# Four pairs of k tiles by seven products in the down groups too, with the buffers that this needs

## The chip, the cores and the metric

The kernel runs on one core of a Trainium2 chip. The metric is the device time of one execution in microseconds (us), the median of several runs. A core has TensorE (PE, with its weight load PEld), VectorE (DVE), ScalarE (ACT), GpSimd (POOL) and SyncE (SP), each with an instruction queue of its own, and 16 DMA engines that they share. SP issues the plain loads here, POOL the transfers that add to what lies in SBUF.

## What is computed

A decoder trunk of two layers over 256 tokens of 2048 features in float32: layer A with native sparse attention, layer B with dilated attention over one shared K/V, both with attention to 256 memory tokens, and each ended by a SwiGLU feed-forward network (FFN) with 5632 hidden features:

```python
def swiglu(h, w_gate, w_up, w_down):
    return (jax.nn.silu(h @ w_gate) * (h @ w_up)) @ w_down

def layer_b(h, ...):          # layer_a alike, with other attention
    ...
    h = h + o                 # o: attention, projected by w_out
    return h + swiglu(rms_norm(h, norm_ffn), w_gate, w_up, w_down)
```

## The kernel before

**Arithmetic.** Each float32 operand is split into a rounded part and a rest (`split`, lines 78 to 85: ScalarE copies to the `hi` tile, VectorE subtracts to the `lo` tile), and a product of two is three matmuls of 128 x 128 by 128 x 512 (`mm3`, lines 87 to 91: hi x hi, hi x lo, lo x hi).

**Groups of the FFN.** The FFN goes through groups that each fill four PSUM banks: two token tiles by two blocks of 512 columns. A gate/up group gives 512 hidden features from 16 k tiles. The eleven of them come in portions of 4, 4 and 3 (`PORTIONS`), and after each portion two down groups take its hidden features (16, 16 or 12 k tiles) to the 2048 outputs and add them to `h`. In layer B the last portion's down part is done without groups. Per layer the order is: b0, b1, b2, b3, two down groups, b4 to b7, two down groups, b8, b9, b10, and the last down part.

**Seven products for eight.** In a group a pair of k tiles is a 2 x 2 product of blocks (token tile x k tile by k tile x column block), which needs eight block products. For the first pairs of a group (`NPX` = 4 in gate/up groups, `NPH` = 3 in the down groups of the first two portions, 2 in those of the last) the kernel takes seven products of sums and differences instead. On the weights' side VectorE and accumulating POOL transfers build the sums from four quarters (`q`, 512 columns for each pair, so 1536 or 2048 columns); on the activations' side `Paired.finish` (lines 281 to 291) builds them once. The other k tiles are plain chunks: one k tile, 12 matmuls, one 512 KB load each (`raw`, four buffers; `whi`, `wlo`, three).

**The interleaving.** `run_groups` runs the plain chunks of one group and, between them, the seven product steps s0 to s6 of the next (`Group.steps`, line 896 on). `spacing(n)` says how many plain chunks stand ahead of each step, by the number n of plain chunks: 16 in b0, which has no pairs, 10 in a down group with three pairs, 8 in a gate/up group. With 8 it is 1, 2, 2, 2, 0, 1, 0. Each step splits its weights to `qhi` and `qlo` (two buffers each) ahead of its matmuls. The quarters lie in three buffers `qa`, `qb`, `qc`; the next group's first quarter goes to `qa`, which is free after the split of s5. `keep` copies a partial sum from PSUM to one of two buffers, and `rest` holds a difference that starts bank 3 in the next group or is added to `h`.

**Turned activations.** `Paired.heads` (lines 309 to 329) transposes the gated product of a gate/up group on TensorE, six ticks into the next group, and puts it into the hidden tile `hThi`/`hTlo`, through a tile `xf` for the pairs (two pairs at once for the first gate/up group of a portion, one for the second, none later). At the entry to an FFN `Paired.turn` (lines 293 to 306) does the same for `h`, one pair at a time, through one buffer `xf`; `residual_block` queues it after a block of the output projection.

**What sets the order.** TensorE's instructions stand in the order written. The other engines' are ordered by the planner from priorities and a cost model; steps wrapped in `urgent` or `high_priority` go ahead. SP's loads go in order, each held until its buffer is free.

Of the kernel before, what the change touches and what calls it, by code (L numbers as in the profile page):

```python
# [8 lines left out]
F32 = mybir.dt.float32  # L9
F32R = mybir.dt.float32r  # L10
BF16 = mybir.dt.bfloat16
AF = mybir.ActivationFunctionType
# [4 lines left out]
P = 128  # L17
T = 256
# [6 lines left out]
NFB = DFF // 512  # L25
PORTIONS = ((0, 4), (4, 8), (8, 11))
NPX = 4
NPH = 3
NSL = 8
XW = NPX * NSL * P + (KT - 2 * NPX) * T  # L30
HW = NPH * NSL * P + (KT - 2 * NPH) * T
# [13 lines left out]
def decoder_trunk(ctx: ExitStack, tc: tile.TileContext, a: dict, out: bass.AP):  # L45
    nc = tc.nc
# [6 lines left out]
    small.tile([P, PADW], F32, name="padw", bufs=1)  # L53
    phase = ctx.enter_context(ExitStack())
    aux_stack = ExitStack()
    fh = fq = fpool = mm_ps = aux_ps = mm_tags = None

    def open_phase(name, mms, auxs):
# [164 lines left out]
        return r  # L223

    def square_sum(ssq, src):
        junk = work.tile([P, 512], F32, tag="rope2", name="junk") if work is not fq else work.tile([P, 512], F32, tag="hb", name="junk", bufs=2)
        nc.scalar.activation(junk, src, AF.Square, accum_out=ssq)

    def new_ssq():
# [29 lines left out]
    class Paired:  # L259
# [33 lines left out]
        def turn(self, nb, k2, spare):  # L293
            k = nb * 4 + k2 * 2
            if k >= 2 * self.npr:
                to_xT(nb, k2, None, self.gain, tuple(v[:, k - 2 * self.npr:k - 2 * self.npr + 2, :].rearrange("p c t -> p (c t)")
                                                     for v in self.R), spare)
                return
            ps = aux_tile(spare)
            for i, (c, tt) in enumerate(((k, 1), (k, 0), (k + 1, 0), (k + 1, 1))):  # L300
                nc.tensor.transpose(ps[:, i * P:(i + 1) * P], h[:, tt, c * P:(c + 1) * P], ident)
            f = fpool.tile([P, 1, 4, P], F32, tag="xf", name="xf")
            for i in range(2):
                nc.scalar.activation(f[:, 0, i * 2:i * 2 + 2, :], ps[:, i * T:(i + 1) * T].rearrange("p (s t) -> p s t", t=P),  # L304
                                     AF.Copy, scale=self.gain(k + i))
            self.finish(k // 2, 1, f)

        def heads(self, j, tok):

            n = min(max(self.npr - 2 * j, 0), 2)  # L310
            fs = []

            def step(tt):
                ps = aux_tile(tt == 1)
                for i in range(4):
                    nc.tensor.transpose(ps[:, i * P:(i + 1) * P], tok[tt][:, i * P:(i + 1) * P], ident)  # L316
                if n > 0:
                    if tt == 0:
                        fs.append(fpool.tile([P, 2, 4, P], F32, tag="xf", name="xf")[:, :n])
                    f = fs[0]  # L320
                    nc.scalar.activation(f[:, :, 1:3, :] if tt == 0 else f[:, :, 0:4:3, :],
                                         ps[:, :n * T].rearrange("p (q c t) -> p q c t", q=n, t=P), AF.Copy)
                    if tt == 1:
                        self.finish(2 * j, n, f)
                if n < 2:
                    r0 = 4 * j + 2 * n - 2 * self.npr
                    d = tuple(v[:, r0:r0 + 4 - 2 * n, tt * P:(tt + 1) * P] for v in self.R)
                    split(d[0], d[1], ps[:, n * T:].rearrange("p (c t) -> p c t", t=P))

            return [urgent(lambda tt=tt: step(tt)) for tt in range(2)]  # L330
# [514 lines left out]
        return op, finish_rstd(ssq, 4)  # L845

    fpool = p2
    fx, f_r = project_out("a_w_out", KT, 6, 2)
    sub.close()
    stack.close()  # L850
# [2 lines left out]
    class Group:  # L853
# [33 lines left out]
        def fetch(self):  # L887
            self.qa = self.load(0)

        def keep(self, b):  # L890
            t = fq.tile([P, 512], F32, tag="keep", name="keep", bufs=2)
            with tc.high_priority(offset=URGENT):
                nc.scalar.activation(t, self.bank[b], AF.Copy)
            return t

        def steps(self, side):
            def s0():
                if self.qa is None:
                    self.fetch()
                self.new(1)  # L900
                self.product(1, 1, self.qa, side, True)
                with tc.high_priority(offset=URGENT):
                    nc.scalar.activation(self.new(0), self.bank[1], AF.Copy)

            def s1():
                self.qb = self.load(1)
                nc.vector.tensor_add(self.qa, self.qa, self.qb)
                self.new(2)
                self.product(2, 7, self.qa, side, True)
                nc.gpsimd.dma_start(self.qb, self.q[2], accum_op=ALU.add)  # L910
                self.p5 = self.keep(2)

            def s2():
                self.qc = self.load(2)
                nc.vector.tensor_add(self.qa, self.qa, self.qc)
                self.product(1, 5, self.qa, side)
                nc.gpsimd.dma_start(self.qa, self.q[3], accum_op=ALU.add)
                u2 = self.keep(1)
                with tc.high_priority(offset=URGENT):
                    nc.vector.tensor_sub(self.bank[2], self.bank[2], u2)  # L920

            def s3():
                self.product(1, 4, self.qb, side)
                self.r = fq.tile([P, 512], F32, tag="rest", name="rest")
                with tc.high_priority(offset=URGENT):
                    nc.vector.tensor_sub(self.r, self.p5, self.bank[1])
                if self.rest_done is not None:
                    self.rest_done(self)

            def s4():  # L930
                self.product(2, 6, self.qc, side)

            def s5():
                self.qb = self.load(3)
                self.product(1, 3, self.qa, side)

            def s6():
                self.product(0, 2, self.qb, side)

            return [s0, s1, s2, s3, s4, s5, s6]  # L940
# [19 lines left out]
    def spacing(n):  # L960


        return {16: (4, 3, 3, 3, 1, 2, 0), 10: (2, 2, 2, 2, 1, 1, 0), 8: (1, 2, 2, 2, 0, 1, 0)}[n]

    def run_groups(groups):
        for i, g in enumerate(groups):
# [23 lines left out]
    def ffn(pre, op, f_r, last):  # L990
        gq, gs = a[pre + "_gu_q"], a[pre + "_gu_s"]
        groups = []
        for pi, (b0, b1) in enumerate(PORTIONS):
            final = pi == len(PORTIONS) - 1
            nk = 4 * (b1 - b0)
            hp = {}

            def hop(pi=pi, nk=nk, final=final, hp=hp):
                if "op" not in hp:
                    x = pair(lambda i: fh.tile([P, HW], F32R, tag=("hThi", "hTlo")[i], name=("hThi", "hTlo")[i]))  # L1000
                    hp["op"] = Paired(x, NPH - final, nk, sums=not (final and pre == "b"))
                return hp["op"]

            def gate_up(g, j, hop=hop):
                hb = []
                for tt in range(2):
                    t = work.tile([P, 512], F32, tag="hb", name="hb", bufs=2)
                    nc.scalar.activation(t, g.bank[tt], AF.Silu, scale=f_r[:, tt:tt + 1])
                    nc.vector.scalar_tensor_tensor(t, g.bank[2 + tt], f_r[:, tt:tt + 1], t, op0=ALU.mult, op1=ALU.mult)
                    hb.append(t)  # L1010
                deferred.extend(at(hop().heads(j, hb), 6, 6))
# [7 lines left out]
            if final and pre == "b":  # L1019
                run_groups(groups)  # L1020
                last([[a["b_w_down_last"][nb, c] for c in range(nk // CK)] for nb in range(4)], hop().xs, nk)
                return
            npr = NPH - final
            dq, ds = a[f"{pre}_dn_q{pi}"], a[f"{pre}_dn_s{pi}"]
            for n2 in range(2):
                def rest_done(g, n2=n2):
# [137 lines left out]
    for j in range(4):  # L1164
# [8 lines left out]
        deferred.extend(at(heads_T(tok, qT), 4, 7))  # L1173
        deferred.extend(at(dil_head(qT, j), 10, 13, 15, 20, 22, 25, 28, 30))
    fpool = pc
    fx, f_r = project_out("b_w_out", 8, 3, 6)
    stack.close()
    phase.close()
# [59 lines left out]
def _pairs(np, w0, w1, nb, npr):  # L1238


    k = w0.shape[0] // P
    w = np.stack([w0.reshape(k, P, nb, 512), w1.reshape(k, P, nb, 512)], 3).transpose(2, 0, 1, 3, 4)
    pr = w[:, :2 * npr].reshape(nb, npr, 2, P, 2, 512)
    q = np.stack([pr[:, :, 0, :, 0], pr[:, :, 0, :, 1], pr[:, :, 1, :, 1], pr[:, :, 1, :, 0]], 1)
    q = np.ascontiguousarray(q.transpose(0, 1, 3, 2, 4)).reshape(nb, 4, P, npr * 512)
    r = np.ascontiguousarray(w[:, 2 * npr:]).reshape(nb, k - 2 * npr, P, 1024)
    return q, r, np.ascontiguousarray(w[0]).reshape(k, P, 1024)
# [28 lines left out]
def _layout(np, i):  # L1276
# [24 lines left out]
    for pre in "ab":  # L1301
        gate, up, wd = i[pre + "_w_gate"][0], i[pre + "_w_up"][0], i[pre + "_w_down"][0]
        q, r, first = _pairs(np, gate, up, NFB, NPX)
        g[pre + "_gu_0"] = first
        g[pre + "_gu_q"], g[pre + "_gu_s"] = q[1:], r[1:]
        for pi, (b0, b1) in enumerate(PORTIONS):
            final = pi == len(PORTIONS) - 1
            w = wd[b0 * 512:b1 * 512].reshape(-1, 2, 2, 512)
            q, r, _ = _pairs(np, w[:, :, 0].reshape(-1, 1024), w[:, :, 1].reshape(-1, 1024), 2, NPH - final)
            if pre == "b" and final:  # L1310
                g["b_w_down_last"] = _blocks(np, wd[b0 * 512:b1 * 512])
            else:
                g[f"{pre}_dn_q{pi}"], g[f"{pre}_dn_s{pi}"] = q, r
# [27 lines left out]
```

## Time and profile before

| what | value |
|---|---|
| median of 3 runs | 2032.63 us (2030.09 to 2034.38) |
| profiled execution: time, span | 2029.28 us, 2027.5 us |
| TensorE busy, matmuls | 2004.9 us (99%), 9363 |
| VectorE, ScalarE, GpSimd busy | 1556.5 (77%), 1208.1 (60%), 63.6 us (3%) |
| mean granted TensorE clock | 0.998 |
| DMA | 457.35 MB, mean 226 GB/s |
| chain that ended last | PE 94%, DVE 2%, DMA 1%, ACT 1% |

Times in the profile are us from the start of the span unless marked ns. A busy share of TensorE includes overlapping matmuls, so that it says little by itself; start times in the timeline do. "Idle" figures name what released the engine, by the semaphore event that came last. Layer A's FFN runs from 417 to about 1111 us, layer B's from 1320 to the end.

### The profile page before, as it was taken

The page shows a single profiled execution, that of the slowest core. Times are in us where ns is not written, and L with a number is a line of the kernel's source. Part 1 is how long each engine was busy: PE and PEld are TensorE (multiplying, and loading weights), DVE is VectorE, ACT ScalarE, POOL GpSimd, SP SyncE. Part 2 cuts the span into 40 slices and gives each one's busy share as a digit, 9 for nine tenths or more (in the row PEclk, how much of TensorE's full clock was granted, in tenths as well). Part 3 has the DMA queues.
Part 4 walks back from the last instruction along what each step waited for, and adds up shares of the span by engine and source line. Part 5 has one row for each costly group of instructions (what it writes and reads, how often), then busy time and mean ns, then how long its engine had stood idle before and what let it go on. Part 6 is the DMA issues. An engine that isn't in the chain of part 4 may idle for free.

```text
span 2027.5 us, 25444 instructions
## 1 busy us (share of the span) xinstructions
PE 2004.9 (99%) x9363; PEld 1665.5 (82%) x9363; DVE 1556.5 (77%) x1942; ACT 1208.1 (60%) x1531; POOL 63.6 (3%) x92
## 2 busy tenths in 40 slices
PE   9999999999999999999999999999999999999998
PEld 7898888888888888888887888878888888888886
DVE  6767798677877788877876678777877788777754
ACT  7755566656655566555665555656655565655643
POOL 0000000000000000000000000000000000000000
PEclk9999999999999999999999999999999999999999
DMA  8867633587878788778875754487777887788754
GB/s 305 278 195 238 218 116 124 177 280 225 264 224 245 242 259 270 222 242 250 264 213 169 236 166 155 147 286 240 247 221 236 261 267 247 213 249 271 227 187 145
DMA packets 107996, 457.35 MB, mean 226 GB/s; under 512 B 12512, under 2 KB 12896, under 8 KB 92128
## 3 DMA queue, kind: packets, MB, share of 16 engines
q1 hardware_dynamic: 98208, 395.31, 56.2%
q0 software_dynamic: 9376, 59.38, 15.4%
q8 instruction: 73, 1.20, 0.2%
q10 hardware_dynamic: 288, 1.05, 0.1%
q14 instruction: 51, 0.42, 0.1%
HBM read 451.50 MB, written 4.19 MB: 225 GB/s over the span
## 4 chain that ended last, share of the span: by engine, by line
PE 94%; DVE 2%; DMA 1%; ACT 1%; issue 0%; SPq 0%; POOLq 0%; POOL 0%; ACTq 0%; DVEq 0%
PE mm L91 30%; PE mm L89 30%; PE mm L90 29%; PE aux L316 1%; PE aux L235 1%; PE aux L91 1%; PE aux L90 1%; DVE qlo L81 1%; PE aux L89 1%; DMA q<-in_b_gu_q_dram 1%; DVE wlo L81 0%; ACT qhi L80 0%; PE aux L350 0%; PE cmp L639 0%; PE cmp L638 0%
## 5 line engine op out<-in xcount | busy, mean ns | idle before, releaser
L80 ACT ACTIVATE whi<-raw 128x1024 fp32r<-128x1024 f32 (+1 forms) x440 | 459.0, 1045 | 372.2 <-PE mm L90 320.8
L81 DVE TENSOR_TENSOR wlo<-raw,whi 128x1024 fp32r<-128x1024 f32 (+1 forms) x440 | 527.6, 1203 | 174.9 <-ACT whi L80 171.5
L81 DVE TENSOR_TENSOR qlo<-q,qhi 128x2048 fp32r<-128x2048 f32 (+2 forms) x210 | 436.1, 2077 | 165.4 <-ACT qhi L80 160.3
L80 ACT ACTIVATE qhi<-q 128x2048 fp32r<-128x2048 f32 (+2 forms) x210 | 366.8, 1747 | 239.8 <-PE mm L90 117.4
L89 PE MATMUL mm<-whi,xhi 128*128 128x512 f32 (+1 forms) x1216 | 472.5, 389 | 3.7 <-ACT xf L304 1.7
L91 PE MATMUL mm<-wlo,xhi 128*128 128x512 f32 (+1 forms) x1216 | 467.7, 385 | 0.0
L90 PE MATMUL mm<-whi,xlo 128*128 128x512 f32 (+1 forms) x1216 | 467.3, 384 | 0.0
L89 PEld LDWEIGHTS mm<-whi,xhi 128*128 128x128 f32 x1216 | 228.4, 188 | 46.8 <-ACT xf L304 2.1
L91 PEld LDWEIGHTS mm<-wlo,xhi 128*128 128x128 f32 x1216 | 228.3, 188 | 46.2
L90 PEld LDWEIGHTS mm<-whi,xlo 128*128 128x128 f32 x1216 | 228.7, 188 | 42.0
L91 PE MATMUL mm<-qlo,xhi 128*128 128x512 f32 x560 | 218.3, 390 | 3.0 <-DVE qlo L81 3.0
L89 PE MATMUL mm<-qhi,xhi 128*128 128x512 f32 x560 | 218.9, 391 | 0.0
L90 PE MATMUL mm<-qhi,xlo 128*128 128x512 f32 x560 | 217.9, 389 | 0.0
L89 PE MATMUL mm<-whi,hThi 128*128 128x512 f32 x480 | 187.6, 391 | 0.0
L91 PE MATMUL mm<-wlo,hThi 128*128 128x512 f32 x480 | 186.9, 389 | 0.0
L90 PE MATMUL mm<-whi,hTlo 128*128 128x512 f32 x480 | 186.8, 389 | 0.0
L84 DVE SCALAR_TENSOR_TENSOR wlo<-raw,gains,whi 128x512 fp32r<-128x512 f32 x160 | 113.9, 747 | 47.6 <-ACT whi L83 47.5
L83 ACT ACTIVATE whi<-raw,gains 128x512 fp32r<-128x512 f32 x160 | 107.6, 716 | 59.4 <-PE mm L90 47.8
L91 PEld LDWEIGHTS mm<-qlo,xhi 128*128 128x128 f32 x560 | 105.1, 188 | 26.2 <-DVE qlo L81 4.2
L89 PEld LDWEIGHTS mm<-qhi,xhi 128*128 128x128 f32 x560 | 105.1, 188 | 21.6 <-ACT qhi L80 0.4
L90 PEld LDWEIGHTS mm<-qhi,xlo 128*128 128x128 f32 x560 | 105.1, 188 | 21.6
L91 PEld LDWEIGHTS mm<-wlo,hThi 128*128 128x128 f32 x480 | 90.1, 188 | 18.7
(280 smaller groups left out, 2424.2 us busy)
## 6 DMA issues: line engine op xcount, KB each, us to landing
q<-in_a_gu_q_dram SPq DMA_DIRECT2D x40, 1024.0 KB, 6.5
raw<-in_a_gu_s_dram SPq DMA_DIRECT2D x80, 512.0 KB, 6.7
q<-in_b_gu_q_dram SPq DMA_DIRECT2D x40, 1024.0 KB, 6.6
raw<-in_b_gu_s_dram SPq DMA_DIRECT2D x80, 512.0 KB, 6.7
raw<-in_a_dn_s_dram SPq DMA_DIRECT2D x56, 512.0 KB, 5.6
q<-in_a_gu_q_dram POOLq DMA_DIRECT2D x20, 1024.0 KB, 9.7
q<-in_b_gu_q_dram POOLq DMA_DIRECT2D x20, 1024.0 KB, 9.8
raw<-in_b_dn_s_dram SPq DMA_DIRECT2D x40, 512.0 KB, 6.0
```

The costliest lines, as they stand in the source:

```text
L80: nc.scalar.activation(hi, src, AF.Copy)
L81: nc.vector.tensor_sub(lo, src, hi.bitcast(F32))
L83: nc.scalar.activation(hi, src, AF.Copy, scale=gain)
L84: nc.vector.scalar_tensor_tensor(lo, src, gain, hi.bitcast(F32), op0=ALU.mult, op1=ALU.subtract)
L89: nc.tensor.matmul(o, l[0], r[0], start=start, stop=False, skip_group_check=more)
L90: nc.tensor.matmul(o, l[1], r[0], start=False, stop=False, skip_group_check=more)
L91: nc.tensor.matmul(o, l[0], r[1], start=False, stop=stop, skip_group_check=more)
L235: nc.tensor.transpose(ps[:, i * P:(i + 1) * P], s, ident)
L316: nc.tensor.transpose(ps[:, i * P:(i + 1) * P], tok[tt][:, i * P:(i + 1) * P], ident)
```

## The change

- `NPH` goes from 3 to 4, and the last portion keeps 2. Down groups of the first two portions have four pairs and 8 plain chunks instead of three and 10, so they use `spacing(8)`; the hidden tile is wider (`HW`).
- The first group of an FFN gets `spacing` 6, 2, 2, 3, 1, 2, 0 instead of 4, 3, 3, 3, 1, 2, 0.
- Turned heads no longer have a tile `xf` of their own: each pair takes one 512-wide buffer of the gated product's tag `hb`, which has three buffers instead of two, and the pairs of a head are copied and finished one by one.
- The two `keep` buffers and `rest` become one buffer `p5`, on which the difference is made in place, and one `u2`.
- `xf` at the entry to the FFN has two buffers in layer A and three in layer B.

```diff
-NPH = 3
+NPH = 4
...
+    xf_bufs = [1]
...
-            f = fpool.tile([P, 1, 4, P], F32, tag="xf", name="xf")
+            f = fpool.tile([P, 1, 4, P], F32, tag="xf", name="xf", bufs=xf_bufs[0])
...
-                if n > 0:
+                for q in range(n):
                     if tt == 0:
-                        fs.append(fpool.tile([P, 2, 4, P], F32, tag="xf", name="xf")[:, :n])
-                    f = fs[0]
-                    nc.scalar.activation(f[:, :, 1:3, :] if tt == 0 else f[:, :, 0:4:3, :],
-                                         ps[:, :n * T].rearrange("p (q c t) -> p q c t", q=n, t=P), AF.Copy)
+                        fs.append(fq.tile([P, 512], F32, tag="hb", name="xf", bufs=3).rearrange("p (q s t) -> p q s t", q=1, s=4))
+                    f = fs[q]
+                    nc.scalar.activation(f[:, 0, 1:3, :] if tt == 0 else f[:, 0, 0:4:3, :],
+                                         ps[:, q * T:(q + 1) * T].rearrange("p (c t) -> p c t", t=P), AF.Copy)
                     if tt == 1:
-                        self.finish(2 * j, n, f)
+                        self.finish(2 * j + q, 1, f)
...
     fpool = p2
+    xf_bufs[0] = 2
...
-        def keep(self, b):
-            t = fq.tile([P, 512], F32, tag="keep", name="keep", bufs=2)
+        def keep(self, b, tag):
+            t = fq.tile([P, 512], F32, tag=tag, name=tag)
...
-                self.p5 = self.keep(2)
+                self.r = self.keep(2, "p5")
...
-                u2 = self.keep(1)
+                u2 = self.keep(1, "u2")
...
-                self.r = fq.tile([P, 512], F32, tag="rest", name="rest")
                 with tc.high_priority(offset=URGENT):
-                    nc.vector.tensor_sub(self.r, self.p5, self.bank[1])
+                    nc.vector.tensor_sub(self.r, self.r, self.bank[1])
...
-        return {16: (4, 3, 3, 3, 1, 2, 0), 10: (2, 2, 2, 2, 1, 1, 0), 8: (1, 2, 2, 2, 0, 1, 0)}[n]
+        return {16: (6, 2, 2, 3, 1, 2, 0), 10: (2, 2, 2, 2, 1, 1, 0), 8: (1, 2, 2, 2, 0, 1, 0)}[n]
...
-                    hp["op"] = Paired(x, NPH - final, nk, sums=not (final and pre == "b"))
+                    hp["op"] = Paired(x, 2 if final else NPH, nk, sums=not (final and pre == "b"))
...
-                    t = work.tile([P, 512], F32, tag="hb", name="hb", bufs=2)
+                    t = work.tile([P, 512], F32, tag="hb", name="hb", bufs=3)
...
     fpool = pc
+    xf_bufs[0] = 3
```

## Rows read from the trace of the kernel before

**Rows 1.** The page, busy us (share) x instructions of TensorE.

```profile
PE 2004.9 (99%) x9363; PEld 1665.5 (82%) x9363; DVE 1556.5 (77%) x1942; ACT 1208.1 (60%) x1531; POOL 63.6 (3%) x92
```

**Rows 2.** Waits of PE: us in total, times, longest us.

```profile
PE mm L91 <- DVE qlo L81: 3.7, 4, 1.6
```

**Rows 3.** Timeline of PE, 600 to 604 us: start us, us, what.

```profile
600.77 0.39 PE L89 MATMUL mm<-whi,hThi 128*128 128x512 f32 x1
...
603.49 0.39 PE L89 MATMUL mm<-whi,hThi 128*128 128x512 f32 x1
```

**Rows 4.** Groups by line and form: busy, mean ns, idle before.

```profile
L81 DVE TENSOR_TENSOR qlo<-q,qhi 128x2048 fp32r<-128x2048 f32 x140 | 320.7, 2291 | 121.1 <-ACT qhi L80 121.1
L80 ACT ACTIVATE qhi<-q 128x2048 fp32r<-128x2048 f32 x140 | 268.5, 1919 | 156.1 <-PE mm L90 92.1 <-DVE q L915 31.5 <-DVE q L907 13.5
...
L81 DVE TENSOR_TENSOR qlo<-q,qhi 128x1536 fp32r<-128x1536 f32 x56 | 98.4, 1757 | 40.7 <-ACT qhi L80 36.0 <-PE aux L316 3.3 <-PE mm L90 1.4
L80 ACT ACTIVATE qhi<-q 128x1536 fp32r<-128x1536 f32 x56 | 83.4, 1489 | 74.7 <-PE mm L90 23.2 <-DVE q L915 16.4 <-DVE q L907 15.4
```

**Rows 5.** Windows, down then gate/up group: PE, PEld, DVE, ACT, POOL, clock, DMA, GB/s.

```profile
604.60:645.30 40.70, 40.70 (x185) 33.79 (x184) 32.23 (x28) 22.59 (x21) 1.76 (x2) 1.00 0.82 259
...
727.60:769.30 41.70, 41.70 (x190) 34.62 (x189) 35.75 (x28) 27.53 (x26) 1.76 (x2) 1.00 0.79 248
```

**Rows 6.** Timelines of SP, ACT and PE, 760 to 777 us.

```profile
765.23 3.05 SPq L875 DMA_DIRECT2D q<-in_a_gu_q_dram  x2
...
771.48 1.92 ACT L80 ACTIVATE qhi<-q 128x2048 fp32r<-128x2048 f32 x1 [1.59 <-DMA q<-in_a_gu_q_dram]
...
774.82 0.39 PE L90 MATMUL mm<-qhi,xlo 128*128 128x512 f32 x1
775.77 0.50 PE L91 MATMUL mm<-qlo,xhi 128*128 128x512 f32 x1 [0.56 <-DVE qlo L81]
```

**Rows 7.** DMA, 510 to 525 us (first line), then 760 to 775 us in slices.

```profile
q<-in_a_gu_q_dram SPq DMA_DIRECT2D x2, 1024.0 KB, 4.8
...
GB/s 415 415 339 448 404 481 426 426 492 371 459 393 339 437 404 426 393 404 437 404 371 426 437 459 371 393 393 481 437 393 350 437 382 361 360 382 164 44 33 0
...
q<-in_a_gu_q_dram SPq DMA_DIRECT2D x2, 1024.0 KB, 6.0
```

**Rows 8.** Timelines of SP, ACT and PE, 1713 to 1725 us.

```profile
1713.98 3.06 SPq L875 DMA_DIRECT2D q<-in_b_dn_q_dram  x2
...
1719.47 1.49 ACT L80 ACTIVATE qhi<-q 128x1536 fp32r<-128x1536 f32 x1 [3.02 <-DMA q<-in_b_dn_q_dram]
...
1723.79 0.39 PE L91 MATMUL mm<-qlo,hThi 128*128 128x512 f32 x1
```

**Rows 9.** Tile xf: duration ns min/median/max, first and last start us, forms.

```profile
L81 DVE TENSOR_TENSOR hTlo<-xf,hThi x19: 681/1218/1226, 491.0 to 1896.8; 128x1024 fp32r<-128x1024 f32 x11, 128x512 fp32r<-128x512 f32 x8
L287 DVE TENSOR_TENSOR xf<-xf x17: 279/292/421, 370.8 to 1686.6; 128x128 f32<-128x128 f32 x12, 128x256 f32<-128x256 f32 x5
```

**Rows 10.** Timelines of DVE and PE, 774 to 796 us.

```profile
781.67 2.29 DVE L81 TENSOR_TENSOR qlo<-q,qhi 128x2048 fp32r<-128x2048 f32 x1
...
784.98 0.39 PE L91 MATMUL mm<-qlo,xhi 128*128 128x512 f32 x1
```

**Rows 11.** Timelines of ACT, DVE, PE and SP, 1306 to 1336 us.

```profile
1319.66 0.82 ACT L304 ACTIVATE xf<-aux,gains 128x256 f32<-128x256 f32 x2
...
1318.77 1.28 DVE L335 TENSOR_TENSOR h<-mm,h 128x512 f32<-128x512 f32 x2
...
1320.54 0.50 PE L89 MATMUL mm<-whi,xhi 128*128 128x512 f32 x1 [1.70 <-ACT xf L304]
...
1325.15 0.80 SPq L875 DMA_DIRECT2D q<-in_b_gu_q_dram  x2
...
1330.67 1.90 ACT L80 ACTIVATE qhi<-q 128x2048 fp32r<-128x2048 f32 x1
...
1334.95 0.50 PE L91 MATMUL mm<-qlo,xhi 128*128 128x512 f32 x1 [1.59 <-DVE qlo L81]
```

More of the change, by code (lines that the diff above doesn't have):

```diff
@@ L225, in square_sum @@
     def square_sum(ssq, src):
-        junk = work.tile([P, 512], F32, tag="rope2", name="junk") if work is not fq else work.tile([P, 512], F32, tag="hb", name="junk", bufs=2)
+        junk = work.tile([P, 512], F32, tag="rope2", name="junk") if work is not fq else work.tile([P, 512], F32, tag="hb", name="junk", bufs=3)
         nc.scalar.activation(junk, src, AF.Square, accum_out=ssq)
@@ L1022, in ffn @@
                 return
-            npr = NPH - final
+            npr = 2 if final else NPH
             dq, ds = a[f"{pre}_dn_q{pi}"], a[f"{pre}_dn_s{pi}"]
@@ L1308, in _layout @@
             w = wd[b0 * 512:b1 * 512].reshape(-1, 2, 2, 512)
-            q, r, _ = _pairs(np, w[:, :, 0].reshape(-1, 1024), w[:, :, 1].reshape(-1, 1024), 2, NPH - final)
+            q, r, _ = _pairs(np, w[:, :, 0].reshape(-1, 1024), w[:, :, 1].reshape(-1, 1024), 2, 2 if final else NPH)
             if pre == "b" and final:
```

## The prediction

> **What bounds the kernel now.** I read the page's busy shares first, then what TensorE waits for, then TensorE's timeline inside a down group. TensorE is busy for 2004.9 of 2027.5 us [rows 1], and the waits on it come to a handful of short stops: the largest kind is four waits for `qlo`, 3.7 us together [rows 2]. A busy share alone doesn't say that the matmuls run back to back, so the timeline is the proof: a plain chunk of a down group is twelve 512-column matmuls, and it starts 2.72 us before the next one, 0.2267 us each, with no idle time marked [rows 3]. The granted clock of both kinds of group is 1.00 [rows 5]. So in the FFN one matmul fewer is worth 0.227 us, unless VectorE, ScalarE or a load comes late in its place. Those are near: VectorE is busy for 35.8 of 41.7 us in a gate/up group and 32.2 of 40.7 us in a down group [rows 5], so what counts is not its total but the order in a burst.
>
> **The matmuls that go.** One more pair takes two k tiles out of the plain part (2 chunks x 12 = 24 matmuls) and puts 7 products x 3 = 21 into the paired part: 3 fewer. It holds for two portions x two groups x two layers = 8 groups: 24 matmuls x 0.2267 = 5.44 us. Nothing lies beside them; this part is sure, as far as TensorE stays fed.
>
> **What feeds them.** In each of the 8 groups, seven splits grow from 1536 to 2048 columns: ScalarE 1.49 to 1.92, VectorE 1.76 to 2.29 us [rows 4]. VectorE: 7 x 0.53, plus two additions of the same size (2 x 0.53), less two plain `wlo` of 1024 columns (1.22 each, the same subtraction as in [rows 9]): 4.8 - 2.4 = +2.3 us. ScalarE: 7 x 0.43 less two `whi`, about +1. With 32.2 + 2.3 = 34.5 of about 40 us a down group becomes as tight on VectorE as a gate/up group is now, and those run with TensorE full. I cost this at nothing; the cover is the 5 to 6 us of VectorE's idle time, and without it the cost would be 2.3 us x 8.
>
> **The first product after a seam of groups.** This is where I expect loss. With `spacing` of 8 the next group's first quarter can be loaded only when product s5 has been split, and product s0 comes one chunk into the next group. At 765.23 SP issues that 1 MB load, ScalarE can split it at 771.48 (6.25 us later, idle until the DMA), `qhi` 1.92 and `qlo` 2.29 follow, and TensorE, which wanted it at 774.82 + 0.23, goes on at 775.77: a stop of 0.72 us [rows 4, 6]. So landings under some 5.5 us cost nothing and each us above costs one. While ScalarE waits for the load, the next chunks' `whi` stand behind it on its queue, so a much later load would stop plain chunks too. In two windows of 15 us over such seams the median landing is 4.8 and 6.0 us [rows 7]. Today layer A and layer B have eight such seams with 1 MB, and two of them stop TensorE: this one and its like in layer B (of the four waits of [rows 2], 3.7 us, 1.6 go to the seam of [rows 11] and 0.6 to this one; the other two share 1.5, so some 0.9 us with the restart). The change makes 16 more: the down groups go from `spacing` 10 to 8 (one chunk less before s0) and their quarters from 768 KB to 1 MB.
> Four are the first down groups of a portion, which follow the gate/up groups. At the tightest SP issues at 1713.98, the split starts at 1719.47, 1.49 + 1.76 later it is ready, 1722.72, and TensorE wants it at 1723.79: 1.07 us to spare [rows 4, 8]. The change takes 0.43 + 0.53 of that for the wider split, and 256 KB more to land. While its engines are 9 tenths busy the DMA moves some 410 GB/s [rows 7], so 0.64 us. The sum is 1.60 against 1.07: 0.5 us lost there. The other three have more to spare; bounds 0 and 0.72 each, and I take 0.2 on average, 0.8 us.
> The Trainium skill (DMA: Bandwidth & Descriptors, Bandwidth, "Where 436 GB/s comes from") says that loads from HBM are bound by the core's share of HBM, about 358 GB/s. By that the 256 KB would take an estimated 0.73 us, and these four seams 0.4 us more in all; the trace disagrees, since the slices of [rows 7] stay above 358 for most of 12 us, so I use the row.
> The other twelve (second down group, and the two gate/up groups after the down groups) have no turned heads ahead of them, which is what made the load late at 765. If they behaved as the eight of today, two stops of 0.7 and 0.9 us in eight, they would cost 12 x 0.2 = 2.4 us; with the shorter landings, 0. I take 0.6, nearer to nothing, since the burst is absent.
>
> **Turned heads.** In portions of gate/up groups the first head now finishes its two pairs one by one: VectorE 2 x 1.22 + 4 x 0.42 = 4.1 us becomes 4 x 0.68 + 8 x 0.29 = 5.0 us [rows 9]. The second head has two pairs instead of one: 2 x 0.68 + 4 x 0.29 = 2.5 more, less two plain subtractions of 256 columns (0.42 each): +1.7 us. They are urgent and stand in front of product s1's `qlo`. Today at the tightest place that `qlo` ends at 781.67 + 2.29 = 783.96 and TensorE reads it at 784.98: 1.0 us to spare [rows 10]. So the first head costs nothing and the second between 0 and 0.7 us, four times; as part of its work can slip behind `qlo`, I take 0.15 each, 0.6 us. The shared buffers cost nothing: three rotate, the fourth tile of a head lands on a buffer whose reader, TensorE's transposition, has ended before the copy can start. `keep` and `rest` merged into single buffers: the old contents are read at the start of a group and written three chunks later, nothing.
>
> **The seams of the layers.** Entering layer B's FFN, TensorE waits until 1320.54 for ScalarE's `xf` copies, which start only at 1319.66 because the one buffer was in use; the additions to `h` that it also needs end at 1318.77 + 1.28 = 1320.05 [rows 11]. With three buffers the copies come early and the additions decide: 0.45 us gained, not the whole stop. The first quarter of the next group is issued at 1325.15 and split at 1330.67, and TensorE stops for 1.59 us (1.76 with the restart) before 1334.95 [rows 11]. The new `spacing` puts that product two chunks, 5.4 us, later: the stop goes whole. Moving s0 moves s1 and its load, addition and accumulating POOL transfer too, by one chunk; s2 to s6 keep their places, and the first group of layer A has several us to spare, so nothing waits for them. At layer A's seam only the additions to `h` end last; two buffers gain 0. Together 2.2 us; bounds 0 and 3.6.
>
> **The sum.** 5.4 + 2.2 - 0.8 - 0.6 - 0.6 = 5.6 us. The profiled execution took 2029.28 us, so it would be 2023.7; the median of the three runs is 2032.63, 3.35 above it, and against that the forecast is 2027.0. A difference under 0.2% (4.1 us) can't be told from none here, so "faster" begins at 2028.5 and "slower" at 2036.7.
>
> **Rivals.** (1) *Landings half way.* The sixteen new seams cost 0.4 us each instead of 0.09: 7.6 - 6.4 - 0.6 = 0.6 gained, 2032.0. For it: the load of [rows 6] is late whenever the transfers before it bunch. Against: six of eight don't stop. (2) *Landings decide every seam, slower.* With 1 MB quarters and no group of ten chunks left, the transfers never catch up, and all sixteen land 6.4 us after issue, little above the 6.25 of [rows 6]: 16 x 0.9 = 14.4 us of stops, less 7.6, plus 0.6: 2040. It turns the sign where sixteen landings average 5.9 us (0.44 us at each eats the 7.0 that are left), and can be measured as slower from 6.2 us. Against: a down group moves 259 GB/s and a gate/up group 248 [rows 5], well under the 410. (3) *The seam gives nothing:* something else, VectorE's additions or the pool's release, still holds entry and first quarter: 5.4 - 2.0 = 3.4, 2029.2. (4) *All of it:* no new stop, and the two at 774 and its like in layer B vanish by a shifted order: 5.4 + 2.2 + 1.6 = 9.2, 2023.4.
>
> **How the numbers follow.** Forecast 2027.0 (its own range 2025.0 to 2028.5) 0.52; (4) 0.10; (3) 0.13; (1) 0.16; (2) 0.09. Faster is the forecast and (4), 0.62; same (3) and (1), 0.29; slower (2), 0.09. The range goes from 2023.0 to 2033.0: it leaves out (2), half of (4) and the outer part of (1).
>
> **What would show it.** Right: 9339 matmuls, chunks still 2.72 us; at layer B's entry the first matmul right after the additions to `h`, and no stop before its first product; stops of `qlo` at the first product of a group, under 1 us, mainly where the down groups begin. Wrong: more than six new such stops, or ScalarE's idle time before `qhi` "until the DMA" above 1.8 us at the down groups; or new stops at plain chunks, which would mean that VectorE's total, not the load, is the limit.

## The result and the profile after

The changed kernel takes 2046.07 us (median of 4 runs, 2043.56 to 2048.51), the kernel before 2031.66 beside it: the ratio is 1.0075, with a 95% interval of 1.0063 to 1.0087. It is 14.4 us slower where 5.6 us faster was forecast. The page, with busy us of the engines, the chain that ended last, and two DMA queues (MB, share of 16 engines):

```profile
span 2041.8 us, 25379 instructions
PE 2007.6 (98%) x9339; PEld 1660.0 (81%) x9339; DVE 1581.7 (77%) x1973; ACT 1223.0 (60%) x1546; POOL 63.7 (3%) x92
...
q1 hardware_dynamic: 95904, 395.31, 55.1%
q0 software_dynamic: 9376, 63.57, 16.2%
...
PE 82%; DVE 8%; DMA 5%; ACT 4%; issue 1%; SPq 0%; POOLq 0%; POOL 0%; ACTq 0%; DVEq 0%
```

The 24 matmuls are gone [rows 1], and the busy time doesn't tell of the loss: TensorE counts 2.7 us more busy with 24 matmuls fewer. The chain does: TensorE's share was 94% and is 82%, and VectorE, DMA and ScalarE have taken its place. The waits (us in total, times, longest) say where, after and, in the last four lines, before:

```profile
PE mm L92 <- DVE qlo L82: 13.6, 12, 1.6
PE aux L302 <- DVE h L336: 1.0, 1, 1.0
...
ACT qhi L81 <- DMA q<-in_b_gu_q_dram: 23.1, 13, 3.0
ACT qhi L81 <- DMA q<-in_a_gu_q_dram: 22.1, 14, 2.9
ACT qhi L81 <- DMA q<-in_a_dn_q_dram: 17.7, 10, 3.1
ACT qhi L81 <- DMA q<-in_b_dn_q_dram: 16.6, 8, 4.2
...
ACT qhi L80 <- DMA q<-in_a_dn_q_dram: 12.1, 6, 2.5
ACT qhi L80 <- DMA q<-in_b_gu_q_dram: 9.8, 9, 2.3
...
ACT qhi L80 <- DMA q<-in_a_gu_q_dram: 8.6, 8, 1.8
...
ACT qhi L80 <- DMA q<-in_b_dn_q_dram: 7.4, 3, 3.0
```

TensorE's four waits for `qlo`, 3.7 us [rows 2], have become twelve, 13.6 us, and ScalarE's idle time before `qhi` "until the DMA" is 79.5 us in the four rows, where those of before add up to 37.9.

As an account of the whole span, take for each 512-column matmul the time to the next start beyond 0.2267 us. The sum is 29.1 us before and 48.7 after: 19.6 more, less 5.4 for the 24 matmuls, is, but for 0.1, the 14.3 us by which the span grew. Of the 48.7 us, 16.3 stand at the first product (s0) of eleven groups; before, two such stops took 1.7 (the one at layer B's entry [rows 11] is counted with the entries below). So nine are new, more than the six that the prediction named as a sign of being wrong. At these eleven the split starts 6.1 to 7.9 us after SP issued the quarter, and at fifteen others, which don't stop, 4.6 to 5.3; the remaining four belong to the first two groups with products in each layer. Another 2.9 us are eight stops of 0.36 us for `qlo` at product s6 of the second down group and of the gate/up group after it; there were none of these before. The entries, told below, give 1.4 back. The rest, 3.5 us, is in small pieces, among them restarts of 0.1 us behind the stops.

Eight of the eleven, 13.8 us, follow a group in which a turned head is finished by pairs, and these are all eight such groups of the first two portions. (The last portions have two more: layer A's is followed by a product of two pairs, which doesn't stop, and layer B's by none.) Here is one of them, from the head to the stop (timelines of DVE, POOL, ACT, SP and PE):

```profile
741.01 1.29 DVE L82 TENSOR_TENSOR hTlo<-xf,hThi 128x512 fp32r<-128x512 f32 x2 [0.51 <-ACT hThi L81]
743.85 2.29 DVE L82 TENSOR_TENSOR qlo<-q,qhi 128x2048 fp32r<-128x2048 f32 x1
...
755.37 0.89 POOL L919 DMA_DIRECT2D q<-in_a_gu_q_dram  x1 [14.48 <-DVE qlo L82]
...
766.44 1.92 ACT L81 ACTIVATE qhi<-q 128x2048 fp32r<-128x2048 f32 x1 [2.55 <-DMA q<-in_a_gu_q_dram]
...
770.71 2.83 SPq L877 DMA_DIRECT2D q<-in_a_gu_q_dram  x2
...
777.77 1.92 ACT L81 ACTIVATE qhi<-q 128x2048 fp32r<-128x2048 f32 x1 [2.63 <-DMA q<-in_a_gu_q_dram]
...
782.07 0.50 PE L92 MATMUL mm<-qlo,xhi 128*128 128x512 f32 x1 [1.60 <-DVE qlo L82]
```

The head's finishing stands on VectorE ahead of s1's `qlo`, which ends at 746.14 and is in time: TensorE reads it at 746.77. But s2's split comes later for it, the accumulating transfer that needs `qa` back from s2 goes out at 755.37, its sum is there for s5 only at 766.44, `qa` is free at 770.7, and the next group's first quarter can be split 7.06 us after its issue, not 6.25 as in [rows 6] (landings are counted to the split that waits for them, as the prediction does it). TensorE stops for 1.77 us, and for 0.56 ahead of the product's first matmul; before, the stop in this place was 0.72. Counted from TensorE's start on product s0 of the same chain (737.26; before, 732.90), the transfer into `qa` goes out after 18.1 us (before: 16.9) and the next first quarter after 33.4 (before: 32.3). So the first quarter is 1.1 us later at its issue and lands 0.8 us more slowly.

Why does it take 7 us? The windows of that stretch (busy us of PE, PEld, DVE, ACT, POOL; clock; DMA's busy share; GB/s):

```profile
737.50:747.50 10.00, 10.00 (x50) 8.38 (x49) 9.49 (x16) 8.46 (x13) 0.88 (x1) 1.00 0.62 127
747.50:757.50 10.00, 10.00 (x45) 8.02 (x44) 9.15 (x6) 6.33 (x6) 0.89 (x1) 1.00 0.63 147
757.50:767.50 10.00, 10.00 (x46) 8.29 (x45) 7.79 (x7) 5.47 (x5) 0.00 (x0) 1.00 0.94 281
767.50:777.50 10.00, 10.00 (x46) 8.29 (x45) 7.04 (x5) 5.48 (x6) 0.00 (x0) 1.00 1.02 422
```

A group moves some 250 GB/s on average, but 127 in its first ten us and 422 in the last ten, with every DMA engine busy. While VectorE works off the head and what stood behind it (9.5 and 9.2 of 10 us busy), no split frees a quarter's buffer, and no quarter goes out between 740.01 and 755.37; then three go out in 6.3 us, plain chunks between them, and the next first quarter is behind them. The granted clock is 1.00 throughout, so TensorE's speed has no part in it. The bunch itself isn't new: in this group the kernel before had 103 and 416 GB/s in its first and last ten us. The change makes it later and the landing behind it longer.

At the entries to the FFN (DVE and PE in layer A, then in layer B):

```profile
373.10 0.69 DVE L336 TENSOR_TENSOR h<-mm,h 128x512 f32<-128x512 f32 x1
...
373.85 0.66 PE L302 MATMUL aux<-ident,h 128*128 128x128 f32 x4 [1.02 <-DVE h L336]
...
1326.56 1.40 DVE L336 TENSOR_TENSOR h<-mm,h 128x512 f32<-128x512 f32 x2
...
1328.11 0.47 PE L90 MATMUL mm<-whi,xhi 128*128 128x512 f32 x1 [0.88 <-DVE h L336]
```

Layer B's entry went as told: the additions to `h` decide, and neither of the two stops of [rows 11] is left as it was (1.86 us is 1.04, 1.76 is 0, 2.6 us gained). In layer A the second buffer has put the finishing of a second pair ahead of an addition to `h` on VectorE, and a transposition waits for it: a stop of 1.2 us that wasn't there.

### The profile page after: what moved, and what is told of

It is laid out like the page before. It is cut to its first block, busy times and chain, and to the rows that moved or that the text cites. A ratio compares the mean times of both kernels' runs of the same rounds, so it can differ in the third digit from the quotient of the medians.

```text
span 2041.8 us, 25379 instructions
## 1 busy us (share of the span) xinstructions
PE 2007.6 (98%) x9339; PEld 1660.0 (81%) x9339; DVE 1581.7 (77%) x1973; ACT 1223.0 (60%) x1546; POOL 63.7 (3%) x92
## 3 DMA queue, kind: packets, MB, share of 16 engines
q1 hardware_dynamic: 95904, 395.31, 55.1%
q0 software_dynamic: 9376, 63.57, 16.2%
## 4 chain that ended last, share of the span: by engine, by line
PE 82%; DVE 8%; DMA 5%; ACT 4%; issue 1%; SPq 0%; POOLq 0%; POOL 0%; ACTq 0%; DVEq 0%
PE mm L92 26%; PE mm L90 25%; PE mm L91 25%; DVE qlo L82 5%; ACT qhi L81 3%; DMA q<-in_b_gu_q_dram 1%; DMA q<-in_a_gu_q_dram 1%; DMA q<-in_b_dn_q_dram 1%; PE aux L317 1%; PE aux L236 1%; DVE wlo L82 1%; DVE h L1039 1%; DMA q<-in_a_dn_q_dram 1%; PE aux L92 1%; PE aux L91 1%
## 5 line engine op out<-in xcount | busy, mean ns | idle before, releaser
L81 ACT ACTIVATE whi<-raw 128x1024 fp32r<-128x1024 f32 (+1 forms) x424 | 442.0, 1044 | 348.1 <-PE mm L91 308.3
L82 DVE TENSOR_TENSOR wlo<-raw,whi 128x1024 fp32r<-128x1024 f32 (+1 forms) x424 | 507.2, 1202 | 150.5 <-ACT whi L81 145.9
L82 DVE TENSOR_TENSOR qlo<-q,qhi 128x2048 fp32r<-128x2048 f32 (+1 forms) x210 | 466.2, 2221 | 183.4 <-ACT qhi L81 183.0
L81 ACT ACTIVATE qhi<-q 128x2048 fp32r<-128x2048 f32 (+1 forms) x210 | 390.6, 1860 | 224.0 <-PE mm L91 111.4
L90 PE MATMUL mm<-whi,hThi 128*128 128x512 f32 x416 | 162.4, 390 | 0.0
L92 PE MATMUL mm<-wlo,hThi 128*128 128x512 f32 x416 | 161.9, 389 | 0.0
L91 PE MATMUL mm<-whi,hTlo 128*128 128x512 f32 x416 | 161.9, 389 | 0.0
L92 PE MATMUL mm<-qlo,hThi 128*128 128x512 f32 x252 | 99.3, 394 | 8.2 <-DVE qlo L82 7.9
```

The lines of the kernel that those rows point to most:

```text
L81: nc.scalar.activation(hi, src, AF.Copy)
L82: nc.vector.tensor_sub(lo, src, hi.bitcast(F32))
L90: nc.tensor.matmul(o, l[0], r[0], start=start, stop=False, skip_group_check=more)
L91: nc.tensor.matmul(o, l[1], r[0], start=False, stop=False, skip_group_check=more)
L92: nc.tensor.matmul(o, l[0], r[1], start=False, stop=stop, skip_group_check=more)
```

## The experiments

Three theories stood. **B**, bunching: the heads hold back the splits that free buffers, the transfers bunch at the end of the group, and the next first quarter lands too late. (In the first expectations it stands in a narrower form, L: a loop through the buffer `qa`.) **V**: VectorE and ScalarE are short of time for the wider splits. **H**: finishing heads pair by pair costs by itself. Ratios are to the kernel before on the same chip.

**An earlier issue of the first quarter.** `qa` and `qc` change roles in every second group, so that the next group's first quarter goes to a buffer that is free after s4.

```diff
+    flips = [i % 2 for i in range(64)]
...
+            self.flip = 0 if quarters is None else flips.pop()
...
-            t = fq.tile([P, QW], F32, tag=("qa", "qb", "qc", "qb")[i], name=("q11", "q12", "q22", "q21")[i])[:, :n]
+            t = fq.tile([P, QW], F32, tag=(("qa", "qb", "qc", "qb"), ("qc", "qb", "qa", "qb"))[self.flip][i], name=("q11", "q12", "q22", "q21")[i])[:, :n]
```

> The changed kernel, with the roles of the buffers qa and qc exchanged in every second group: the next group's first quarter is loaded into the buffer that is free after the split of s4, not after that of s5, some 8 us earlier. Same instructions, same sizes. Theory L (a loop through qa: load 7, split 4.2, addition 2.3, split 4.2, addition 2.3, split 4.2, accumulating transfer 10, split 4.2 us, 38 to 39 us in a group of 41, which the heads' work makes longer than the group): the stops at the first products, 16 us in all, go; 2031 us or less. Theory V (VectorE and ScalarE are simply short of time with wider splits): 2046, the stops move elsewhere. Theory H (the heads finished pair by pair cost it by themselves): 2046.

Measured: 2029.59 us, ratio 0.9994 (0.9984 to 1.0003), 16.5 us less than the changed kernel. SP, then ACT:

```profile
761.24 0.33 SPq L880 DMA_DIRECT2D q<-in_a_gu_q_dram  x1
...
773.28 1.92 ACT L81 ACTIVATE qhi<-q 128x2048 fp32r<-128x2048 f32 x1 [1.42 <-PE mm L91]
```

The load goes out 8 us before the split of s5 has freed the other buffer (769.40), and the split of s0 waits for TensorE to give back a buffer, no longer for the DMA. VectorE's and ScalarE's work is the same to the instruction count (1973 and 1546), so V can't be the cause of the stops at first products, nor H by itself. No first product stops any more; five stops of 0.3 to 1.4 us at product s2 are left.

**Three pairs again**, with the new heads and all else.

```diff
-NPH = 4
+NPH = 3
```

> The changed kernel with NPH back at 3: heads pair by pair, shared buffers, the new spacing and the turn buffers stay. Theory L: the down groups with ten chunks have time to spare for the loop again, and the stops stay only where they were before, slightly longer for the first heads: 2030 to 2032 us. Theory V: 2030. Theory H: the first heads (two pairs, one by one, in five of eleven portions' groups with pairs) still cost, 2038.

Measured: 2033.30, ratio 1.0015 (1.0005 to 1.0024). 12.8 us come back, a little less than L had: four first products behind heads stop even with three pairs, some 6 us together where two took 1.7, the one at 782 us for 1.76. Beyond the turn buffers and the new spacing this kernel has only the new heads and the merged buffers, so I put these stops down to the longer heads; the merged buffers (`p5`, `u2`) were not tried by themselves.

**Heads two pairs at once**, with four pairs.

The pairs share one tile `xf` again; to make room, `hb` has two buffers and `u2` rotates through them.

```diff
-                for q in range(n):
+                if n > 0:
...
-                        self.finish(2 * j + q, 1, f)
+                        self.finish(2 * j, n, f)
...
-                u2 = self.keep(1, "u2")
+                u2 = self.keep(1, "hb", 2)
```

> The changed kernel, with the turned heads copied and finished two pairs at once in a tile of their own, as before the change (hb has two buffers again, and u2 rotates through them to make room). Four pairs stay. Theory H: 2029 us. Theory L: the heads' VectorE work falls from 5.0 to 4.1 us, and with it each of some ten stops by 0.9 us at most: 2037 to 2042. Theory V: 2044.

Measured: 2034.26, ratio 1.0013 (1.0004 to 1.0023). Better than L had, 11.8 us instead of 4 to 9; the stops behind the heads fall from between 0.6 and 2.3 us to between nothing and 1.1.

**Heads later**, behind the split of s2.

```diff
-                ps = aux_tile(tt == 1)
+                ps = aux_tile(spare and tt == 1)
...
-                deferred.extend(at(hop().heads(j, hb), 6, 6))
+                deferred.extend(at(hop().heads(j, hb, j >= 2), *((30, 40) if j < 2 else (6, 6))))
```

> The changed kernel, with the first two turned heads of a portion at ticks 30 and 40 of the next group, behind the split of s2 and its accumulating transfer, instead of both at tick 6, ahead of the split of s1 (both then use the one auxiliary PSUM bank). Theory L: the transfer into qa starts 3 to 5 us earlier and s5 is split in time: stops fall to 1 us or less, 2033 us. Theory V: 2046. Theory H: about 2046, the work is the same.

Measured: 2028.77, ratio 0.9986 (0.9976 to 0.9996). Better than L's 2033. The same head work, moved, takes 17.3 us off. The same group as above, its windows, and then SP and ACT at its end:

```profile
734.70:744.70 10.00, 10.00 (x46) 8.28 (x45) 9.05 (x6) 6.33 (x6) 0.87 (x1) 1.00 0.58 122
744.70:754.70 10.00, 10.00 (x48) 8.27 (x47) 7.72 (x5) 6.65 (x8) 0.88 (x1) 1.00 0.95 230
754.70:764.70 10.00, 10.00 (x48) 8.27 (x47) 8.22 (x14) 7.28 (x9) 0.00 (x0) 1.00 0.98 379
764.70:774.70 10.00, 10.00 (x46) 8.29 (x45) 9.30 (x11) 7.61 (x8) 0.00 (x0) 1.00 0.77 273
...
767.18 3.33 SPq L877 DMA_DIRECT2D q<-in_a_gu_q_dram  x2
...
771.96 1.92 ACT L81 ACTIVATE qhi<-q 128x2048 fp32r<-128x2048 f32 x1 [1.95 <-DMA q<-in_a_gu_q_dram]
```

The transfers start earlier, the last ten us move 273 GB/s instead of 422, and the first quarter, issued at the same point of the chain (counted from s0 as above, after 32.7 us instead of 33.4), lands in 4.78 us instead of 7.06. This is what turned L into B. A second reason lies in the changed kernel: in the group before the stop at 824 us s5's split waits for TensorE and not for a transfer, so it isn't late, and the landing alone, 7.3 us, makes the stop (ACT and SP):

```profile
810.06 1.92 ACT L81 ACTIVATE qhi<-q 128x2048 fp32r<-128x2048 f32 x1 [1.66 <-PE mm L91]
...
814.33 3.05 SPq L877 DMA_DIRECT2D q<-in_a_dn_q_dram  x2
...
821.63 1.92 ACT L81 ACTIVATE qhi<-q 128x2048 fp32r<-128x2048 f32 x1 [2.65 <-DMA q<-in_a_dn_q_dram]
```

**Less traffic**, to test the landing by itself.

```diff
-                self.qb = self.load(3)
```

> The changed kernel without the plain load of the fourth quarter (product s6 takes what still lies in qb; the result of the paired k tiles is therefore not the reference's). One of the six quarter transfers of a group goes, 1 MB of 10, and it is the one issued after s3, in the crowded part; every split, addition, head and matmul stays. Theory B (the heads delay the splits that free buffers, the transfers bunch at the end of the group, and the next first quarter, last in line, lands 7 us after its issue instead of 5): it lands in 5 us, the stops go, 2031 us. Theory V (VectorE's and ScalarE's time or order ahead of s0): 2046, as nothing there changes. A loop through qa and its accumulating transfer alone: between, some 2040, since that transfer and the splits stay.

Measured: 2028.39, ratio 0.9985 (0.9976 to 0.9995). SP and ACT in the same group:

```profile
768.81 2.53 SPq L877 DMA_DIRECT2D q<-in_a_gu_q_dram  x2
...
773.68 1.91 ACT L81 ACTIVATE qhi<-q 128x2048 fp32r<-128x2048 f32 x1 [0.74 <-DMA q<-in_a_gu_q_dram]
```

With 1 MB less ahead of it the quarter lands in 4.87 us, and 17.7 us are gone with every head, split and matmul in place. Counted from s0 as above, it is issued after 33.3 us, 33.4 in the changed kernel, so little but the landing has changed here. Three first products still stop, 0.5 to 0.9 us each, and there the split starts 6.0 to 6.4 us after the issue. The edit also takes away the wait of s6's split for the load that is gone; that split ended 7 us ahead of s0's in the changed kernel, so it isn't what held s0. B holds; the narrower loop would have left some 2040.

**Both cures, and one turn buffer again in layer A.** Two kernels, the second also without `xf_bufs[0] = 2`:

> Both cures together: qa and qc exchanged in every second group, and the first two heads at ticks 30 and 40. Theory L (one loop, which either cure breaks): what one has cured the other can't cure again; only the stops that each left (0.6 to 1.4 us at product s2 with the exchange, 0.5 to 0.7 us at a few first products with late heads) go: 2026 us. If the two cured different things, the gains over the changed kernel would add: 16.5 + 17.3, 2012, which the 24 matmuls' kernel cannot reach.

Measured: 2025.52, ratio 0.9974 (0.9964 to 0.9984). As expected, the cures don't add: they cure one thing.

> As the first of these four, with one turn buffer again at layer A's entry. The stop at 374 us, 1.2 us, goes: 2025 us, if the additions to h stand ahead of the second pair again.

Measured: 2024.12, ratio 0.9968 (0.9956 to 0.9980). The stop at 374 us is gone. This kernel beats both, and its chain and waits are TensorE's again:

```profile
PE 94%; DVE 4%; ACT 1%; DMA 0%; issue 0%; SPq 0%; POOLq 0%; POOL 0%; DVEq 0%; ACTq 0%
...
PE mm L90 <- DVE h L336: 0.9, 1, 0.9
PE mm L92 <- DVE qlo L82: 0.8, 1, 0.8
```

**The same edits on the kernel before.** First the turn buffers and the new spacing alone, then the exchange alone, then the late heads alone:

> The kernel before with two and three turn buffers and the new spacing of the first group, nothing else. My prediction: 2.2 us faster, all at layer B's entry. From the trace of the changed kernel: layer B's entry gives 0.8 + 1.8, but layer A's two buffers put a stop of 1.2 us before a transposition at 374 us, where VectorE finishes a second pair ahead of the addition to h: 1.4 us faster in all.

Measured: 2030.25, ratio 0.9998 (0.9989 to 1.0007): 1.1 us by the medians, too little to be told from none.

> The kernel before, with qa and qc exchanged in every second group. Theory L: its two stops at first products behind the heads (0.7 and 1.0 us) go, little else: 1.5 us faster. If the exchange itself is a gain whatever the loop, it is as large here as in the changed kernel, 16 us.

Measured: 2028.94, ratio 0.9990 (0.9981 to 0.9999).

> The kernel before with its first two heads of a portion at ticks 30 and 40. Theory B: its two stops at first products (0.7 and 1.0 us) go, nothing else: 1.5 us faster. If the late place is a gain by itself, as large as in the changed kernel: 17 us.

Measured: 2030.37, ratio 0.9998 (0.9988 to 1.0007). The two stops behind heads are gone in both traces, where the same line is left of TensorE's waits for `qlo` (four, 3.7 us, in [rows 2]):

```profile
PE mm L91 <- DVE qlo L81: 2.4, 2, 1.6
```

The time moves by at most 2.4 us: neither edit gains by itself what it gains in the changed kernel.

So against the turn buffers and spacing alone (2030.25), the new heads with the merged buffers cost some 3 us with three pairs, four pairs cost 3 to 4 us with the old heads (the 5.4 us that they save included), and both together some 16; each of these is good to 2 or 3 us. That is more than their sum: each eats spare time, and the stops begin where none is left.

## Why the prediction was wrong, step by step

- *The matmuls that go*: right. 9339 matmuls, still 0.227 us apart, 5.4 us. The kernel with both cures and one turn buffer agrees: 5.4, 2.6 at layer B's entry and 1.7 at the two old first products, less 2.9 at product s6, make 6.8 us, and it is 7.2 faster than the kernel before.
- *What feeds them*, nothing: nearly right. With the first quarter issued earlier, the same VectorE and ScalarE work runs at 2029.59. But the eight waits for `qlo` at product s6, 2.9 us, came with the fourth pair and stay with both cures.
- *The first product after a seam*, 1.4 us: the step that failed. Its price was right (a landing above some 5.5 us stops TensorE by the excess), and so was one of its places, "mainly where the down groups begin": the four first down groups have 7.6 us of the stops. But I priced a landing there as today's plus 256 KB at 410 GB/s, 0.2 us of stop each; it was 1.5 to 2.2 us, with landings of 7.0 to 7.9 us, 4.5 to 5.5 before, because the landing depends on what is in the line ahead of it. For the other twelve I took 0.6 us, "since the burst is absent"; that was near, one of them stops, 1.1 us. What the sum doesn't have at all is that the eight seams of before could get worse: six of them stop, 7.6 us, where two took 1.7. The Trainium skill (DMA: Bandwidth & Descriptors, Bandwidth) gives about 358 GB/s for a core when both cores of a pair stream. This kernel runs on one core, and its trace shows 422 GB/s for ten us, above the limit that the prediction quoted.
- *Turned heads*, 0.6 us: the other half of the failure. I followed the head only to the next reader, s1's `qlo`, which had 1.0 us to spare and still has 0.6. What it delayed was s2's split, the buffers behind it and with them the transfers. The cost came thirty us later, at the next group's s0, and was 13.8 us with what stood there before.
- *The seams of the layers*, 2.2 us: layer B gave 2.6 in the trace, nearly right; layer A's "two buffers gain 0" missed the 1.2 us stop that the second buffer makes. By itself the whole edit could not be told from no gain.
- *Rivals*: the second, landings at every seam, 2040, had the late landing and the sign, and I gave it 0.09. That its time was near is in part luck: it has all sixteen new seams stop, for want of groups of ten chunks, and five do, 8.8 us; the other six stops are at old seams. What I held against it was the average, 259 and 248 GB/s against 410 [rows 5]. The average of a group says nothing of the last ten us; the windows of a quarter group would have. These are the first and the last of the kernel before, in the same group as above:

```profile
732.00:742.00 10.00, 10.00 (x50) 8.38 (x49) 8.27 (x6) 6.50 (x8) 0.87 (x1) 1.00 0.49 103
...
762.00:772.00 10.00, 10.00 (x46) 8.29 (x45) 7.04 (x5) 6.03 (x7) 0.00 (x0) 1.00 1.02 416
```

## What to carry to other kernels

When work is put in front of a split that frees a buffer, follow the chain to the next load and to the transfers queued with it, not only to the next reader. Cost a load by what is in line when it is issued, from windows of a fraction of the loop; the loop's mean rate hides a bunch. Where a buffer's release makes the last load late, another buffer that is free earlier may do: here two buffers changed roles, and it cost no memory.

## What the runs showed of the hardware

The packets of the accumulating transfers take the DMA engines longer than their bytes tell: 16.2% of the engines' time for 63.57 MB on POOL's queue against 55.1% for 395.31 MB on SP's (the page above), 1.8 times as much for a MB. In the first two windows of the changed kernel above the engines are busy for 0.62 and 0.63 of the time while only 127 and 147 GB/s move.
